# A sixth pair of up-projections with seven products, in a layer bound by TensorE

## The chip, the cores and the metric

The kernel runs on one core of one Trainium2 chip. The metric is the device time of one launch in microseconds (us), the median of several runs. TensorE (PE) does the matrix products, VectorE (DVE) and ScalarE (ACT) prepare operands and drain results, GpSimd (POOL) does some elementwise work and issues some DMAs, SyncE (SP) issues most DMAs.

## The reference, cut to what matters

One layer is computed for 512 tokens of width 1024: forgetting attention with 16 heads, a layer norm, a gated FFN with a causal convolution, a second layer norm, and a gated embedding. All of it is float32. The change sits in the FFN's first product and in what is done for it ahead of time.

```python
def conv_ffn(x, w_up, conv_w, conv_b, w_down):
    u, g = jnp.split(x @ w_up, [FFN_DIM], axis=-1)      # FFN_DIM = 2816 = 22 slices of 128
    g = causal_dwconv(g, conv_w, conv_b)                # 3 taps along the tokens
    return (jax.nn.gelu(g, approximate=False) * u) @ w_down
...
mix = fox_mixer(x, ...)                                 # q, k, v, forget gate; 16 heads
x = layer_norm(ALPHA * x + mix, ...)
x = layer_norm(ALPHA * x + conv_ffn(x, ...), ...)
x = x + sigmoid(x @ ple_w_gate + ple_b_gate) * (p @ ple_w_proj)
```

## The kernel before

**Products.** Every float32 product is made of three matmuls in a rounded format: each operand is cut into a high and a low part, and `three` (L152) adds high-high, high-low and low-high. A weight unit of up to 128x1024 is loaded into a `raw` buffer, ACT copies it to `whi` (L123), DVE subtracts to get `wlo` (L129). `W.get(i, ahead)` cuts all units up to i + ahead and starts their loads; the five `whi`/`wlo` buffers take turns.

**Stages.** V is projected in three groups of heads (`value_rows(0)` to `(2)`), with the forget gate's running sum `cr` between groups 0 and 1. Then come the loop over heads (h = 0 to 17, two steps behind the last head to drain), the output projection and the first norm. After that the 22 slices of the FFN are done as 11 pairs j = 0 to 10; slice f has a gate product g and an up product u. Between the steps of a pair PE does pieces ("chunks") of the down projection of earlier pairs, whose sums are called x, y and z, in two buffers each (x00, x01). The second norm and the embedding gate end the kernel.

**Pairs with seven products.** A plain pair (function `up`) does g and u of both slices with moving operands of 512 columns: 4 products of 8 slices of the width, 3 matmuls each, 96 in all. A pair listed in `UP_PAIRS` treats the two slices and the two halves of the width and of the tokens as a 2x2 block product and does seven half-size products instead of eight: `up_step` runs steps st = 0 to 3 for s = 0 (g) and s = 1 (u), with 256 columns, 56 x 3 = 168 matmuls. For this the weights are needed in added and subtracted form. Pairs in `KEPT` have these sums made ahead, while the heads run: `keep_load` loads the two weight blocks `ka` and `kb` and stores the sums of the previous ones to DRAM, `keep_sums` makes four subtractions on DVE (L489 to L492). `ka` has one buffer, so the next load waits for the last store; `kb` takes one of the `raw` buffers. Each pair has two sets, q = 0 and 1.

In a step, ACT and DVE move partial results from PSUM to the buffer `E` and to a corner called `side`. Step 0 of u ends with a DVE addition into `side` (L852, `side<-u,side`), without which step 1 of u cannot start, since it goes on in the same bank. After the last step `conv_product` does the convolution on ACT and DVE (L789 to L792) and the gelu and product (L797, L798). `operand_sums` (L885 to L888, four DVE additions) and `operand_parts` (L893, L894) prepare the results as operands of the down projection. For pairs in `APART`, the last two are done for the pair before, inside step 0 of this pair's u.

**Order.** From slice 2 of the FFN on, the order of DVE and ACT is the order in which the code is written; each engine works through its instructions in order. Before that a scheduler places the instructions by readiness. A numbered name is one tile: whi80 is the high part of the weight unit 80.

The lines that hold PE back are in these functions:

Of the kernel before, what the change touches and what calls it, by code (L numbers as in the profile page):

```python
# [24 lines left out]
KD = D // P  # L25
# [5 lines left out]

CHUNKS = (None, (1,) * 12, (1,) * 12, (2, 1) * 4)

UP_PAIRS = (2, 3, 4, 6, 7, 9)

KEPT = (3, 4, 6, 7)

DMA_PAIRS = (1, 2)

APART = (2, 3, 4, 7)  # L40
HALF = S // 2
ALPHA = 2.0 ** 0.25
EPS = 1e-5
# [99 lines left out]
def trunk_layer(ctx: ExitStack, tc: tile.TileContext, xT, x2d, pT, w0, wqk, wv1, wv2, bf, wo, wup, cwb,  # L143
                wdn, wpl, wg, bg, gm, bm, gf, bff, out):
    nc = tc.nc
# [21 lines left out]
    W = Weights(tc, base)  # L167
# [117 lines left out]
    u_up, u_dn = {}, [[] for _ in PAIRS]  # L285
# [87 lines left out]
    def cut_x(k, c=slice(0, S)):  # L373
        if k == 1 or c.stop == HALF:
            nc.vector.tensor_copy(xh[:, k, c], xraw[k][:, c])
        else:
            nc.scalar.activation(xh[:, k, c], xraw[k][:, c], AF.Copy)
        return nc.vector.tensor_sub(xl[:, k, c], xraw[k][:, c], xh[:, k, c].bitcast(F32)).ins
# [17 lines left out]

    proj = {}

    def value_rows(n):
        h0, nh = V_HEADS[n]  # L400
        w = VF if n == 0 else wv[n].shape[1]
        pv = [bank(f"pv{t}_{n}") for t in range(NT)]
        if n == 0:
            for s in range(2):
                proj[0, s] = bank(f"pp0_{s}")
        for k in range(KD):
            if n == 0:
                if k + 4 < KD:
                    load_x(k + 4)
                if 0 < k < KD - 1:  # L410
                    cut_x(k + 1)
                hi, lo = W.get(u_0[k + 1])
                c = slice(0, VF)
            else:
                u, c = u_v[n, k]
                hi, lo = W.get(u)
            def some(ts):
                for t in ts:
                    tk = slice(t * P, (t + 1) * P)
                    three(pv[t][:, :w], hi[:, c], lo[:, c], xh[:, k, tk], xl[:, k, tk], k == 0,  # L420
                          k == KD - 1, weights_move=True)

            def first_pair(qh, ql, c0, b):
                for s in range(2):
                    a = slice(c0 + s * P, c0 + (s + 1) * P)
                    three(proj[0, s][:, b], qh[:, a], ql[:, a], xh[:, k, b], xl[:, k, b],
                          k == 0 and b.start == 0, k in (0, KD - 1), lo_first=k > 0,
                          on=k > 0 or b.start > 0)

            if n == 0 and k == 0:  # L430
                qh, ql = W.parts[u_0[0]]
                for i in range(2):
                    first_pair(qh, ql, 0, slice(i * HALF, (i + 1) * HALF))
                    some((2 * i, 2 * i + 1))
            else:
                some((0,))
                if n == 0:
                    first_pair(hi, lo, VF, slice(0, S))
                some((1, 2, 3))
            if n == 0 and k == 0:  # L440
                with tc.issue_after(cut_first):
                    cut_x(1)
        for t in range(NT):
            if n == 0:
                logits[t] = fl_all[:, t * H:t * H + H]
                nc.scalar.activation(logits[t], pv[t][:, nh * DH:w], AF.Copy)
            v = V[:, t, h0:h0 + nh]
            p3 = pv[t][:, :nh * DH].rearrange("p (h d) -> p h d", d=DH)
            nc.scalar.activation(v[:, :, 0, :], p3, AF.Copy)
            nc.vector.tensor_sub(v[:, :, 1, :], p3, v[:, :, 0, :].bitcast(F32))  # L450
# [13 lines left out]

    to_keep, in_work, made, last_sum, last_mask = list(kept.items()), [], [], [], []

    def keep_load():

        if made:
            to, ab = made.pop()  # L470
            for n, t in enumerate(ab):
                nc.sync.dma_start(to[:, 2 * n:2 * n + 2, :], t.rearrange("p (a b) -> p a b", b=512))
        if to_keep:
            (j, q), to = to_keep.pop(0)
            ab = (ap.tile([P, UNIT], F32, name=f"ka{j}_{q}", tag="keep", bufs=1),
                  base.tile([P, UNIT], F32, name=f"kb{j}_{q}", tag="raw", bufs=RAW_BUFS))
            for n, t in enumerate(ab):
                nc.sync.dma_start(t.rearrange("p (a b) -> p a b", b=P), wup[2 * j + n, 1 - q])
            in_work.append((to, ab))
# [158 lines left out]

    stack(0)
    keep_load()  # L640
    value_rows(1)
    stack(1)
    keep_sums()
    keep_load()
    value_rows(2)
    for h in range(H + 2):
        m, s = divmod(h, 2)
        if h == 2:
            project(2, 0)
        if h < H:  # L650
            scores(h)

            if s == 0 and h != 2:
                keep_sums()
                keep_load()
        if m + 1 < KD and h != 2:
            project(m + 1, s)
        for k in OUT_FIRST.get(h, ()):
            out_first(k)
        if s == 1 and h + 1 < H:  # L660
            stack(h + 1)
        if 1 <= h < H + 1:
            turn(h - 1)
        if h >= 2:
            values(h - 2)
        if s == 1 and h + 1 < H:
            stack(h + 2)
        if h == H:
            y = base.tile([P, NT, D], F32, tag="xh", name="y")
            for t in range(NT):  # L670
                nc.sync.dma_start(y[:, t, :], x2d[t * P:(t + 1) * P, :])
# [150 lines left out]
    def up_step(j, st, s, E, amid=None):  # L822
# [4 lines left out]
            ups[j, s] = bank(f"{'gu'[s]}{2 * j}", "two" if j > 2 else None)  # L827
        ps = ups[j, s]
        z, x = ps[:, :HALF], ps[:, HALF:]
        hi, lo = W.get(u_up[j, st, s], 4)  # L830
        first, second = slice(0, HALF), slice(HALF, S)

        def go(to, col, on, a=None, sn=None, last=4):
            for k in range(4):
# [4 lines left out]
                    mh, ml = [v[:, a[0] + k, a[1]] for v in (x1h, x1l)]  # L839
                three(to, hi[:, w], lo[:, w], mh, ml, k == 0 and not on, k == 3, on=on)  # L840

        e = E[:, (1 - s) * 2 * S:(2 - s) * 2 * S]
        c1 = side(7)[:, s * HALF:(s + 1) * HALF]
        if st == 0:
            go(z, 1, False, a=(4, first))
            go(x, 0, True, a=(0, first))
            nc.scalar.activation(c1, z, AF.Copy)
            nc.scalar.activation(z.rearrange("p (a b) -> p a b", b=P),
                                 zeros.unsqueeze(1).to_broadcast([P, 2, P]), AF.Copy)
            if amid is not None:  # L850
                amid()
            nc.vector.tensor_add(c1 if j in APART else e[:, :HALF], x, c1)  # L852
        elif st == 1:
            go(z, 0, True, sn=0)
            go(x, 1, True, sn=1)
            nc.scalar.activation(e[:, S:S + HALF], x, AF.Copy)
            nc.scalar.activation(e[:, S + HALF:], z, AF.Copy)
            if j in APART:
                nc.scalar.activation(e[:, :HALF], c1, AF.Copy)
        elif st == 2:  # L860
            go(z, 1, True, sn=3)
            go(x, 0, True, sn=2)
            nc.vector.tensor_add(e[:, S:], ps, e[:, S:])
        else:
            go(x, 0, True, a=(4, second))
            del ups[j, s]
            nc.scalar.activation(e[:, HALF:S], x, AF.Copy)

    def conv_product(fs, E):

# [370 lines left out]
```

## Time and profile before

| | |
|---|---|
| runs | 645.18, 645.60, 645.79 us; median 645.6 us |
| the profiled execution | 645.37 us; its span in the trace 643.5 us |
| PE busy | 638.3 us of the span, 3635 matmuls, granted clock 1.00 |
| DVE busy | 532.4 us, 863 instructions |
| ACT busy | 383.4 us, 682 instructions |
| POOL busy | 127.6 us |
| DMA | 121.08 MB, mean 188 GB/s |

Times below are in us from the start of the span. A row of the timeline gives start, duration, engine, line, operation and the tiles written and read; "x2" means two instructions drawn as one row. In brackets stands the idle time of the engine before it and what ended it. Durations of successive instructions on one engine overlap in the trace, so the work of a chain is the distance between starts. Busy time in a window says how much an engine did there.

### The profile page before, as it was taken

The numbers are of one execution on the slowest core, as the hardware profiler recorded it, in microseconds if no ns is written. First come the engines' busy times: TensorE is split into PE (matmuls) and PEld (weight loads), VectorE is DVE, ScalarE is ACT, GpSimd is POOL, SyncE is SP. The second block draws the span as 40 slices with busy tenths as digits, with TensorE's granted clock in tenths as the row PEclk, the third lists the DMA queues.
The fourth block names the chain that finished last, engine by engine and source line by source line (L and its number), as shares of the span: only waits on it lengthen the run. The fifth ranks groups of instructions, "written<-read, shape, count | busy, mean of one in ns | idle before, by whom it ended". The sixth has DMA issues, their size and how long they took to land.

```text
span 643.5 us, 10085 instructions
## 1 busy us (share of the span) xinstructions
PE 638.3 (99%) x3635; PEld 560.6 (87%) x3635; DVE 532.4 (83%) x863; ACT 383.4 (60%) x682; POOL 127.6 (20%) x147
## 2 busy tenths in 40 slices
PE   9999999999999999999999999999999999999997
PEld 7899888888888889989999988999988998888886
DVE  6576778988888599857899987889897998699997
ACT  6274777877785326945757563647555455336872
POOL 2000554454456043110000010101011001002001
PEclk9999999999999999999999999999999999999999
DMA  8763625454588387684676838765746764782732
GB/s 314 249 226 117 209 80 185 160 189 155 177 272 321 129 256 215 135 215 156 202 221 158 227 125 250 192 205 149 238 132 202 193 217 115 164 276 61 232 109 98
DMA packets 49393, 121.08 MB, mean 188 GB/s; under 512 B 4864, under 2 KB 7936, under 8 KB 49344
## 3 DMA queue, kind: packets, MB, share of 16 engines
q1 hardware_dynamic: 44400, 107.21, 49.8%
q0 software_dynamic: 4800, 13.11, 11.0%
q8 instruction: 28, 0.46, 0.3%
q14 instruction: 21, 0.17, 0.1%
q10 hardware_dynamic: 144, 0.13, 0.1%
HBM read 107.72 MB, written 18.87 MB: 197 GB/s over the span
## 4 chain that ended last, share of the span: by engine, by line
PE 97%; DMA 1%; DVE 1%; ACT 0%; issue 0%; SPq 0%; DVEq 0%
PE g L152 18%; PE u L152 18%; PE pp L152 14%; PE x L152 8%; PE pv L152 7%; PE pl L152 7%; PE z L152 4%; PE r L152 3%; PE ap L152 3%; PE o L593 3%; PE t L580 2%; PE ao L152 2%; PE y L152 2%; PE s L543 2%; PE s L545 2%; DMA y<-x2d 1%
## 5 line engine op out<-in xcount | busy, mean ns | idle before, releaser
L123 ACT ACTIVATE whi<-raw 128x1024 fp32r<-128x1024 f32 (+4 forms) x136 | 128.1, 945 | 95.0 <-PE pv L152 17.9
L129 DVE TENSOR_TENSOR wlo<-raw,whi 128x1024 fp32r<-128x1024 f32 (+4 forms) x131 | 140.0, 1076 | 27.9 <-ACT whi L123 27.2
L567 POOL TENSOR_SCALAR pr<-pr,rl 128x128 f32<-128x128 f32 (+1 forms) x64 | 75.5, 1194 | 128.1 <-DVE rl L563 125.6
L281 POOL COPY neghalf<-neghalf 128x1 f32<-128x1 f32 x16 | 9.0, 563 | 247.1 <-ACT neghalf L280 247.1
L152 PE MATMUL g<-x1h,whi 128*128 128x256 f32 (+1 forms) x168 | 54.7, 325 | 0.0
L152 PE MATMUL g<-x1l,whi 128*128 128x256 f32 (+1 forms) x168 | 54.4, 324 | 0.0
L152 PE MATMUL g<-x1h,wlo 128*128 128x256 f32 (+1 forms) x168 | 54.3, 324 | 0.0
L152 PE MATMUL u<-x1l,whi 128*128 128x256 f32 (+1 forms) x160 | 52.9, 331 | 0.0
L152 PE MATMUL u<-x1h,wlo 128*128 128x256 f32 (+1 forms) x160 | 52.9, 331 | 0.0
L152 PE MATMUL u<-x1h,whi 128*128 128x256 f32 (+1 forms) x160 | 52.9, 331 | 0.0
L152 PE MATMUL pp<-xh,whi 128*128 128x512 f32 (+1 forms) x130 | 50.7, 390 | 0.0
L152 PE MATMUL pp<-xl,whi 128*128 128x512 f32 (+1 forms) x130 | 50.7, 390 | 0.0
L152 PE MATMUL pp<-xh,wlo 128*128 128x512 f32 (+1 forms) x130 | 50.5, 390 | 0.0
L559 ACT ACTIVATE pr<-s,nm 128x128 f32<-128x128 f32 (+1 forms) x64 | 33.5, 527 | 9.1 <-DVE nm L555 8.9
L152 PEld LDWEIGHTS g<-x1h,whi 128*128 128x128 f32 x168 | 31.9, 190 | 3.4 <-issue 0.7
L152 PEld LDWEIGHTS g<-x1l,whi 128*128 128x128 f32 x168 | 31.9, 190 | 2.7
L152 PEld LDWEIGHTS g<-x1h,wlo 128*128 128x128 f32 x168 | 31.9, 190 | 2.6
L152 PEld LDWEIGHTS u<-x1l,whi 128*128 128x128 f32 x160 | 30.4, 190 | 3.0
L152 PEld LDWEIGHTS u<-x1h,whi 128*128 128x128 f32 x160 | 30.4, 190 | 3.0
L152 PEld LDWEIGHTS u<-x1h,wlo 128*128 128x128 f32 x160 | 30.4, 190 | 2.8
L123 ACT ACTIVATE whi<-side 128x512 fp32r<-128x512 f32 (+1 forms) x33 | 25.5, 782 | 10.4 <-PE u L152 3.6
L555 DVE CUSTOM_DVE_ANT_0 s<-s,mask 128x128 f32<-128x128 f32 (+1 forms) x64 | 30.1, 510 | 1.7 <-PE s L545 1.5
(636 smaller groups left out, 1870.9 us busy)
## 6 DMA issues: line engine op xcount, KB each, us to landing
raw<-wup SPq DMA_DIRECT2D x34, 512.0 KB, 9.1
raw<-wdn SPq DMA_DIRECT2D x23, 512.0 KB, 6.7
raw<-wqk SPq DMA_DIRECT2D x14, 512.0 KB, 5.8
ka<-wup SPq DMA_DIRECT2D x8, 512.0 KB
kb<-wup SPq DMA_DIRECT2D x8, 512.0 KB, 4.3
kept<-kb SPq DMA_DIRECT2D x8, 512.0 KB, 3.2
kept<-ka SPq DMA_DIRECT2D x8, 512.0 KB
raw<-wo SPq DMA_DIRECT2D x8, 512.0 KB, 4.9
```

Of the source, the lines that this page charges most:

```text
L123: self.nc.scalar.activation(hi[:, c:e], piece, AF.Copy)
L129: self.nc.vector.tensor_sub(lo[:, c:e], piece, hi[:, c:e].bitcast(F32))
L152: nc.tensor.matmul(ps, lhsT, rhs, start=start and n == 0, stop=stop and n == 2, skip_group_check=on)
L281: with tc.issue_after(nc.gpsimd.tensor_copy(small[:, m + 32:m + 33], small[:, m:m + 1]).ins):
L543: nc.tensor.matmul(ps[:, :n], QA[:, q], KA[:, :n], start=True, stop=False)
L545: nc.tensor.matmul(ps[:, :n], qb[0:68, q], kb[0:68, :n], start=False, stop=True)
L555: last_mask[:] = [nc.vector.tensor_tensor_reduce(ps[:, :w], ps[:, :w], mask[:, S - w:], -1.0, BIG, op0=ALU.add, op1=ALU.min, accum_out=nm[ ...
L559: nc.scalar.activation(pr[:, off:off + w], ps[:, :w], AF.Exp, bias=nm[:, i:i + 1], scale=-1.0, accum_out=ls[:, i:i + 1])
L567: nc.gpsimd.tensor_scalar_mul(pr[:, off:off + w], pr[:, off:off + w], rl[:, i:i + 1])
L580: nc.tensor.transpose(ps[:, w:w + P], pr[:, o:o + P], ident)
L593: nc.tensor.matmul(ps[:, q0:], V[:, j, h], p[:, o:o + w], start=j == 0 and n == 0, stop=j == NT - 1 and n == 1)
```

## The change

Pair 5 gets seven products: it joins `UP_PAIRS` and `KEPT`, and pairs 5 and 6 join `APART`. Pair 5 then has 168 matmuls of 256 columns in place of 96 of 512; over the kernel PE has 3707 matmuls instead of 3635. Two more sets of sums have to be made and stored ahead. For them sums and loads are issued in the middle of V's second group and right behind it (the stores there go to POOL's queue instead of SP's), and again in the loop at h = 16. Further, `up_step` no longer cuts the unit four ahead at its start but three ahead; the fourth is cut by `ready()` at the step's end, behind the step's copies out of PSUM.

```diff
-UP_PAIRS = (2, 3, 4, 6, 7, 9)
-KEPT = (3, 4, 6, 7)
+UP_PAIRS = (2, 3, 4, 5, 6, 7, 9)
+KEPT = (3, 4, 5, 6, 7)
...
-APART = (2, 3, 4, 7)
+APART = (2, 3, 4, 5, 6, 7)
...
-    def value_rows(n):
+    def value_rows(n, amid=None):
...
+            if amid is not None and k == KD // 2:
+                amid()
...
-    def keep_load():
+    def keep_load(queue=nc.sync):
...
-                nc.sync.dma_start(to[:, 2 * n:2 * n + 2, :], t.rearrange("p (a b) -> p a b", b=512))
+                queue.dma_start(to[:, 2 * n:2 * n + 2, :], t.rearrange("p (a b) -> p a b", b=512))
...
-    value_rows(1)
+    def keep_amid():
+        keep_sums()
+        keep_load(nc.gpsimd)
+
+    value_rows(1, keep_amid)
     stack(1)
-    keep_sums()
-    keep_load()
+    keep_amid()
     value_rows(2)
...
             if s == 0 and h != 2:
                 keep_sums()
                 keep_load()
+        elif s == 0:
+            keep_sums()
+            keep_load()
...
-        hi, lo = W.get(u_up[j, st, s], 4)
+        hi, lo = W.get(u_up[j, st, s], 3)
...
+        def ready():
+            W.get(u_up[j, st, s], 4)
...
+            ready()        # behind the copies of each of the four steps
```

Three places show what this does to the order. Lines of the new kernel are shifted: its keep sums are L491 to L494, its V copies L452, and L864, L881, L900 to L903 are the old L852, L867, L885 to L888.

**V's second group, DVE.** ka3_1 and kb3_1 are the second set of weights of pair 3; fb, fc and cr belong to the forget gate; KA and QB are heads 0 and 1; pv0_1 is the first bank of V's second group. DVE before, from the forget gate's chain on:

```order
L629 TENSOR_TENSOR fb_407<-fb_407,fa_406 16x512
L633 SCALAR_TENSOR_TENSOR fc_421<-fb_407,fz_419 16x512
L634 CAST cr_405<-fc_421 16x512
L530 TENSOR_TENSOR KA0_428<-pp0_1_154,KA0_428 64x512
L635 TENSOR_TENSOR cr_405<-fc_421,cr_405 16x512
L636 TENSOR_SCALAR cr_405<-cr_405 16x512
L637 TENSOR_SCALAR cr_405<-cr_405 16x512
L528 SCALAR_TENSOR_TENSOR QB0_391<-pp0_0_153,QA0_427 64x512
L530 TENSOR_TENSOR KA1_568<-pp0_1_154,KA1_568 64x512
L129 TENSOR_TENSOR wlo15_747<-raw15_521,whi15_746 128x1024
L528 SCALAR_TENSOR_TENSOR QB1_392<-pp0_0_153,QA1_567 64x512
L450 TENSOR_TENSOR V_111<-pv0_1_441,V_111 128x5x64
```

In the changed kernel DVE has L491, L492 (the first two sums of this set), wlo14 and the subtraction on fb in this order, and then:

```order
L493 TENSOR_TENSOR kb3_1_526<-kb3_1_526,ka3_1_525 128x512
L635 SCALAR_TENSOR_TENSOR fc_423<-fb_409,fz_421 16x512
L532 TENSOR_TENSOR KA0_430<-pp0_1_156,KA0_430 64x512
L636 CAST cr_407<-fc_423 16x512
L494 TENSOR_TENSOR ka3_1_525<-ka3_1_525,kb3_1_526 128x512
L637 TENSOR_TENSOR cr_407<-fc_423,cr_407 16x512
L638 TENSOR_SCALAR cr_407<-cr_407 16x512
L639 TENSOR_SCALAR cr_407<-cr_407 16x512
L530 SCALAR_TENSOR_TENSOR QB0_393<-pp0_0_155,QA0_429 64x512
L532 TENSOR_TENSOR KA1_580<-pp0_1_156,KA1_580 64x512
L129 TENSOR_TENSOR wlo15_759<-raw15_533,whi15_758 128x1024
L452 TENSOR_TENSOR V_113<-pv0_1_443,V_113 128x5x64
```

Two sums now stand ahead of wlo14 and two inside the chain from fb to wlo15, and QB1 has moved behind the copies of pv0_1 to pv2_1. On PE the first matmul of pv3_2, the fourth bank of V's third group, waited for QB1 to free its bank; now it waits for the copy of pv0_1. The first matmul of pv2_2 waits for KA1 in both.

**The start of pair 5, DVE.** E4 is pair 4's result, a9 and a8 its two slices, g10 and u10 the banks of pair 5, y the running sum of the down projection. Before, pair 5 is plain, and pair 4's sums follow at once on its last product on DVE:

```order
L798 TENSOR_TENSOR E4_3880<-a8_4113,E4_3880 128x512
L885 TENSOR_TENSOR E4_3880<-E4_3880 128x256
L886 TENSOR_TENSOR E4_3880<-E4_3880 128x256
L887 TENSOR_TENSOR E4_3880<-E4_3880 128x256
L888 TENSOR_TENSOR E4_3880<-E4_3880 128x256
L894 TENSOR_TENSOR a4l_4122<-E4_3880,a4h_4121 128x512
L894 TENSOR_TENSOR b4l_4124<-E4_3880,b4h_4123 128x256
L894 TENSOR_TENSOR s4l_4126<-E4_3880,s4h_4125 128x1024
```

In the changed kernel the same last product is followed on DVE by wlo80 and the step's own addition `side<-g10`, and then:

```order
L223 TENSOR_TENSOR side_2728<-side_2728 128x512
L129 TENSOR_TENSOR wlo81_4190<-raw81_4109,whi81_4189 128x1024
L699 TENSOR_TENSOR y_2406<-y_2406,x00_3478 128x512
L699 TENSOR_TENSOR y_2406<-y_2406,x01_3479 128x512
L699 TENSOR_TENSOR y_2406<-y_2406,z00_3476 128x512
L699 TENSOR_TENSOR y_2406<-y_2406,z01_3477 128x512
L129 TENSOR_TENSOR wlo82_4239<-side_2728,whi82_4238 128x512
L900 TENSOR_TENSOR E4_3902<-E4_3902 128x256
L901 TENSOR_TENSOR E4_3902<-E4_3902 128x256
L902 TENSOR_TENSOR E4_3902<-E4_3902 128x256
L903 TENSOR_TENSOR E4_3902<-E4_3902 128x256
L864 TENSOR_TENSOR side_2728<-u10_4211,side_2728 128x256
```

Ahead of `side<-u10` there now stand three cuts of weights, the addition for g, one subtraction, four additions to y and pair 4's four sums.

**The end of pair 4, ACT.** a9 and a8 are the convolution's first tap (new L797, old L789). Before:

```order
L123 ACTIVATE whi78_4070<-raw78_3976 128x1024
L867 ACTIVATE E4_3880<-g8_3780 128x256
L123 ACTIVATE whi79_4090<-raw79_3994 128x512
L867 ACTIVATE E4_3880<-u8_3836 128x256
L789 ACTIVATE a9_4109<-E4_3880,cw_2437 128x512
L789 ACTIVATE a8_4113<-E4_3880,cw_2437 128x512
L797 ACTIVATE a9_4109<-a9_4109 128x512
```

In the changed kernel, the same place on ACT:

```order
L881 ACTIVATE E4_3902<-g8_3802 128x256
L123 ACTIVATE whi78_4105<-raw78_3998 128x1024
L881 ACTIVATE E4_3902<-u8_3858 128x256
L123 ACTIVATE whi79_4125<-raw79_4041 128x512
L797 ACTIVATE a9_4132<-E4_3902,cw_2459 128x512
L797 ACTIVATE a8_4136<-E4_3902,cw_2459 128x512
L805 ACTIVATE a9_4132<-a9_4132 128x512
```

The cut of unit 79 (512 columns here) has moved from ahead of the copy of u8 to behind it, so it stands between that copy and the convolution; the cut of unit 78 has moved behind the copy of g8.

More of the change, by code (lines that the diff above doesn't have):

```diff
@@ L859, in up_step @@
                 nc.scalar.activation(e[:, :HALF], c1, AF.Copy)
+            ready()
         elif st == 2:
@@ L863, in up_step @@
             nc.vector.tensor_add(e[:, S:], ps, e[:, S:])
+            ready()
         else:
@@ L867, in up_step @@
             nc.scalar.activation(e[:, HALF:S], x, AF.Copy)
+            ready()
     def conv_product(fs, E):
```

## The prediction

> **What bounds the kernel now.** I read the page's busy table and its chain first, then windows cut at the pairs, then the timelines of PE, DVE and ACT around the three places of the change. Busy table and chain:
>
> ```profile
> PE   638.3 (99%) x3635; PEld 560.6 (87%) x3635; DVE 532.4 (83%) x863; ACT 383.4 (60%) x682; POOL 127.6 (20%) x147
> ...
> PE 97%; DMA 1%; DVE 1%; ACT 0%; issue 0%; SPq 0%; DVEq 0%
> ```
>
> PE is busy for 99% of the span and carries 97% of the chain. Every matmul less is time saved, and every wait of PE is time lost. So the question is what PE has to do in pair 5, and whether DVE, the next busiest, still delivers in time. The windows of pairs 4, 5, 6 and 9 (window, its length; busy time and instructions of PE, PEld, DVE, ACT, POOL; clock; DMA share; GB/s):
>
> ```profile
> 342.82:373.94 31.12, 31.12 (x218) 29.16 (x217) 27.80 (x39) 19.42 (x34) 2.43 (x4) 1.00 0.74 197
> 373.94:402.79 28.85, 28.85 (x129) 23.58 (x128) 23.32 (x34) 14.18 (x22) 3.06 (x4) 1.00 0.62 180
> 402.79:433.90 31.11, 31.11 (x218) 29.14 (x216) 26.11 (x38) 17.13 (x30) 2.91 (x4) 1.00 0.67 200
> 493.84:530.39 36.55, 36.55 (x241) 33.65 (x240) 35.92 (x56) 20.23 (x34) 2.22 (x4) 1.00 0.66 192
> ```
>
> In each of them PE is full. A pair with seven products loads DVE to 84 or 89%, pair 9 to 98% without PE stopping. So on average DVE has room in pair 5; what can go wrong is a single wait, at the place where DVE's work is bunched.
>
> **The products of pair 5.** What a matmul costs is the distance of starts:
>
> ```profile
> 51.55 0.28 PE L152 MATMUL pv<-whi,xh 128*128 128x256 f32 x1
> ...
> 51.91 0.28 PE L152 MATMUL pv<-whi,xh 128*128 128x256 f32 x1
> ...
> 380.32 0.39 PE L152 MATMUL x<-whi,s2l 128*128 128x512 f32 x1
> ...
> 382.13 0.39 PE L152 MATMUL u<-x1h,whi 128*128 128x512 f32 x1
> ```
>
> Three starts of 256 columns take 0.36, so 0.120 each; the last two rows are eight starts of 512 columns apart, 1.81 or 0.2267 each. 96 x 0.2267 = 21.76 leaves and 168 x 0.120 = 20.16 comes: **-1.60**. Plain pair 5 also stops once:
>
> ```profile
> 389.61 0.39 PE L152 MATMUL x<-whi,b1h 128*128 128x512 f32 x1
> 389.97 0.47 PE L152 MATMUL g<-x1h,whi 128*128 128x512 f32 x1
> 390.27 0.40 PE L152 MATMUL g<-x1l,whi 128*128 128x512 f32 x1
> ```
>
> These starts are 0.36 and 0.30 apart instead of 0.23, where g of the second slice waits for the bank that the first slice's convolution frees; with seven products this wait is not there: **-0.2**. The price of 256 columns is more than half that of 512 (0.529), which the trace includes. The Trainium skill ("TensorE: Matmul & The Clock Gate", "Wait — 56ns, not 53.3ns?") gives the start-to-start time as columns over 2.4 GHz and some 2.5 ns, an estimate of 0.1092 for 256 columns and 0.2158 for 512; by it the products would gain 2.4. The rows have 0.120, so here the page is too good, and the sum goes by the rows.
>
> **The kept sums in V's second group.** One set costs four DVE instructions (line, engine; ns min/median/max):
>
> ```profile
> L489 DVE TENSOR_TENSOR ka<-kb,ka x8: 684/685/686, 26.6 to 193.3; 128x512 f32<-128x512 f32 x8
> ...
> L492 DVE TENSOR_TENSOR ka<-ka,kb x8: 681/682/879, 30.5 to 197.6; 128x512 f32<-128x512 f32 x8
> ```
>
> about 0.7 each. Where they now stand, DVE before did this:
>
> ```profile
> 41.41 1.22 DVE L129 TENSOR_TENSOR wlo<-raw,whi 128x1024 fp32r<-128x1024 f32 x1 [0.83 <-ACT whi L123]
> 43.88 0.68 DVE L629 TENSOR_TENSOR fb<-fb,fa 16x512 f32<-16x512 f32 x1 [1.24 <-ACT fa L628]
> ...
> 48.98 0.69 DVE L530 TENSOR_TENSOR KA<-pp,KA 64x512 fp32r<-64x512 f32 x1
> 49.70 1.23 DVE L129 TENSOR_TENSOR wlo<-raw,whi 128x1024 fp32r<-128x1024 f32 x1
> 50.96 0.69 DVE L528 SCALAR_TENSOR_TENSOR QB<-pp,QA 64x512 fp32r<-64x512 f32 x1
> 51.69 1.29 DVE L450 TENSOR_TENSOR V<-pv,V 128x320 fp32r<-128x320 f32 x3
> ```
>
> From 43.88 on DVE has no gap. PE's first matmul on pv3_2 is the 51.91 row above; it needed QB1, done at 50.96 + 0.69 = 51.65, so its slack was 0.26. In the new order the first two sums fall into the idle 0.83 and 1.24; the other two lie in the gapless chain and move wlo15 from 49.70 to 51.10. The V copy of pv0_1 follows at 52.36 and takes about 0.5 (1.29 for three, overlapped); PE goes on at some 52.9: **+0.95**. Its lower bound is 0.5, if rows of the chain overlap more than before; nothing leaves it. The first scores come about 10 us later and have slack, so nothing repeats it. KA1 moves to 51.07, still ahead of pv2_2 at 51.55.
>
> This holds if ka3_1 is there when DVE comes to it. L491 may start as late as 43.88 - 1.14 - 2 x 0.7 = 41.3 (1.14 is the distance of two cuts in a row). Its load and the store that it waits for, and landing times of the kept blocks and of all raw loads (same 512 KB):
>
> ```profile
> 31.25 0.33 SPq L472 DMA_DIRECT2D kept<-ka  x1
> ...
> 36.63 0.33 SPq L478 DMA_DIRECT2D ka<-wup  x1
> ...
> DMA to landing us min/median/max: 3.0/3.2/4.3
> ...
> DMA to landing us min/median/max: 2.9/4.8/9.1
> ```
>
> With the kb loads' row (the first, nearest: same source and queue) it lands by 39.8 to 40.9, in time; with the raw loads' median at 41.4, just late; with 9.1 at 45.7, which would cost 4.4 more. The store goes to POOL's queue now. On it the stores of `out`, half that size, land so:
>
> ```profile
> DMA to landing us min/median/max: 1.8/2.3/2.5
> ```
>
> Twice that is 4.6, less than the 5.4 between the two SP rows above, so POOL's queue is not expected to be later. I take 0.05 for this, bounds 0 and 1.0. The Trainium skill has a rule against this move ("SBUF — State Buffer", "SBUF: two separate sides"): a DMA issued by GpSimd has its descriptors written there, and certain DVE operations lock it out meanwhile. Its victims would be these stores; no row before shows a POOL store beside a full DVE, so it stands as a reason for the late-load rival below.
>
> **The start of pair 5.** PE's order there is g step 0, 12 matmuls of a chunk, u step 0, 20 of g step 1, 6 of x, 4 of g, 6 of x, then u step 1: 72 x 0.120 + 24 x 0.2267 = 14.1 after the pair's start T (373.94 before). DVE must have done `side<-u10` by then. Rows for the chain:
>
> ```profile
> 341.87 1.14 ACT L123 ACTIVATE whi<-side 128x512 fp32r<-128x512 f32 x2
> ...
> 348.80 0.36 ACT L847 ACTIVATE side<-g 128x256 f32<-128x256 f32 x1
> ...
> 349.52 1.04 ACT L123 ACTIVATE whi<-raw 128x1024 fp32r<-128x1024 f32 x1
> ...
> 378.34 0.64 ACT L797 ACTIVATE a<-a 128x512 f32<-128x512 f32 x1 [0.81 <-DVE a L792]
> ...
> 353.41 0.42 DVE L885 TENSOR_TENSOR E<-E 128x256 f32<-128x256 f32 x1
> ...
> 354.87 0.42 DVE L852 TENSOR_TENSOR side<-u,side 128x256 f32<-128x256 f32 x1
> ...
> 379.01 0.69 DVE L798 TENSOR_TENSOR E<-a,E 128x512 f32<-128x512 f32 x1 [0.16 <-ACT a L797]
> ...
> 385.91 1.27 DVE L691 TENSOR_TENSOR y<-y,x 128x512 f32<-128x512 f32 x2
> ...
> 388.30 0.74 DVE L790 SCALAR_TENSOR_TENSOR a<-g,cw,a 128x511 f32<-128x511 f32 x1
> ```
>
> Pair 4's last gelu starts at T + 4.4 and, with the cut of unit 79 now ahead of the convolution (half of 1.14), at T + 5.0. Copy, zeroing and whi80 follow on ACT: 0.57 + 0.72 + 1.0 gives T + 7.3. DVE, idle since its last product (T + 6.3), then does wlo80 (1.14, T + 8.4), the addition for g (0.34), a subtraction (0.6) and wlo81 (1.14, T + 10.5), four y additions (388.30 - 385.91 = 2.4, T + 12.9), wlo82 (0.6), four sums (354.87 - 353.41 = 1.46, T + 15.0) and L852 (0.42): T + 15.4 by these distances, some 0.2 less if the last gelu overlaps. Against 14.1 that is a stall of 1.1 to 1.3; I take **+1.1**, bounds 0.3 (ACT keeping its old pace and the idle second of DVE gone) and 1.5. In pair 4 the same wait was met by DVE at 354.87 + 0.42 = 355.3 for a start of u step 1 at 342.82 + 14.1 = 356.9, 1.6 early: there the y additions stood behind it. The four y additions and the idle time are the difference.
>
> **`ready()` in the other pairs.** It moves half a cut to a whole one (0.55 to 1.04) ahead of the convolution, so the same chain is later by as much; pair 4's slack of 1.6 covers 0.55 to 1.04. Pairs 3, 6 and 7 are alike in DVE load, pair 9 is the fullest and was already near its limit. In turn PE's copies out of PSUM come earlier by the same. I take **+0.2** for all, bounds -0.3 and +1.0.
>
> **Sums at h = 16, the loads and stores.** Four more sums of pair 7 lie in a stretch where DVE has gaps of over 2 us: 0, as long as those gaps stay. Pair 5's loads grow by 1.5 MB over 29 us, about 52 GB/s above the 180 in its window; pairs 4 and 6 ran with 197 and 200: 0, and if a cut comes late it adds to the stall at the start of the pair. Pair 5's parts, now inside pair 6's step 0, follow the pattern of pairs 3 and 4: 0.
>
> **Sum.** -1.60 - 0.2 + 0.95 + 0.05 + 1.1 + 0.2 = +0.5. On the profiled execution's 645.37 that is 645.9; this execution stands 0.23 under the median of 645.6, so the median becomes 646.1.
>
> **Rivals.**
> - *DVE keeps up, faster.* Scheduling slack that I count as lost isn't: in pair 5 the four y additions don't hold u10 up, V's stall is half, and the earlier copies out of PSUM help by the lower bound above. For it speaks pair 9, which runs DVE at 98% without stopping PE; against it that 0.26 of slack can't take two sums of 0.7. -1.8 + 0.5 - 0.3 = -1.6: 644.0. It decides in pair 5: if `side<-u10` ends by T + 14.1.
> - *The late load, slower.* ka3_1 lands after 41.3, because its store waits on POOL's queue; all of DVE's chain and V's third group stand behind L491. One us late is one us of PE: 647.1 at one, 648.1 at two. By the page's rule on descriptors this is what would happen. Against it: the first store is at about 31, well ahead of the gapless stretch.
> - *Nothing gained, nothing lost.* Pair 5's products gain 1.6 and its own stall takes just this, with V's stall hidden by later waits of PE: 645.6. PE's few waits in the trace speak against hidden slack.
>
> **Chances.** The forecast with its bounds, 0.54; DVE keeps up 0.18; late load, or the other pairs stalling as well, 0.22; nothing gained 0.06. What a measurement of this kernel can tell from no change is about 0.2%, 1.3 us. Faster by more (under 644.3): most of the second case, 0.13, and 0.04 of the first. Slower by more (over 646.9): the third case's 0.20 and 0.07 of the first. Within: 0.56. The range leaves out one in ten at either end: 644.1 to 647.6.
>
> **What would show it.** The window of V's second group: a PE gap of about 1 us at the first matmul on pv3_2, ended by a V copy. Pair 5: 168 matmuls of 256 columns and 30 of 512 (28.85 - 21.76 - 0.2 is 30 x 0.2267) make 27.0, and beside them a stall of about 1 at u step 1, ended by DVE L864. No new gap over 0.3 in pairs 3, 4, 6, 7, 9. A load of ka landing after 41.3, or gaps in several pairs, would prove it wrong upward; a pair 5 of 27 us with no gap, downward.

## The result: 7.3 us slower

The changed kernel took 652.93 us (median of four runs, 652.34 to 653.99) against 645.64 us before: ratio 1.0116, 95% interval 1.01 to 1.0132. 646.1 had been predicted, with a range up to 647.6. The page of the changed kernel, PE's busy time and its chain:

```profile
PE 639.7 (98%) x3707; PEld 564.0 (87%) x3707; DVE 541.0 (83%) x879; ACT 388.8 (60%) x700; POOL 128.5 (20%) x151
...
PE 85%; DVE 9%; ACT 2%; issue 2%; DMA 1%; DVEq 0%; ACTq 0%
```

The span grew from 643.5 to 650.8. PE had 97% of the chain and has 85% now, DVE 9%. What PE waits for, all of it (engine and line, what ended the wait, us in total, times, longest):

```profile
PE u L152 <- DVE side L864: 3.2, 5, 1.3
PE warm L334 <- DVE zeros L330: 1.1, 1, 1.1
PE g L152 <- ACT side L858: 1.1, 2, 0.6
PE g L152 <- ACT E L881: 0.7, 1, 0.7
PE pv L152 <- DVE V L452: 0.5, 1, 0.5
```

Only the `warm` wait at the start was there before. The largest entry is the addition that ends step 0, and it occurs five times, not once. The waits are rounded down here, since a waiting matmul's predecessor still counts as busy; the distance of starts shows more. Windows from the first matmul of a pair to that of the next, pair 2 before, then pairs 2, 4, 5, 6 and 7 of the changed kernel:

```profile
291.55:311.70 20.15, 20.15 (x169) 20.14 (x168) 15.33 (x22) 12.74 (x22) 0.00 (x0) 1.00 0.59 196
...
293.01:315.53 22.52, 20.61 (x169) 20.25 (x168) 14.14 (x21) 11.48 (x21) 0.00 (x0) 1.00 0.46 154
346.65:378.23 31.58, 31.38 (x218) 29.23 (x217) 27.60 (x39) 19.74 (x35) 2.46 (x4) 1.00 0.74 199
378.23:407.65 29.42, 27.78 (x201) 25.76 (x199) 23.74 (x35) 17.44 (x34) 2.43 (x4) 1.00 0.68 204
407.65:440.30 32.65, 31.65 (x216) 29.19 (x217) 30.50 (x44) 20.40 (x36) 2.46 (x4) 1.00 0.68 205
440.30:471.86 31.56, 31.37 (x218) 29.23 (x217) 27.60 (x39) 19.73 (x35) 2.43 (x4) 1.00 0.69 195
```

Pair 2, where no weight and no product was changed, takes 22.52 instead of 20.15: 2.4 of the 7.3 are lost there. Pairs 4 and 7 take 0.45 more each, pair 6 1.55 more, and pair 5, which should be 1.8 shorter, is 0.6 longer. Up to V's end 1.4 are lost (the sum of all starts that come later than 0.120 and 0.2267 and the like ask: 2.72 before, 4.13 now), but only 0.8 of it where the change is, at pv3_2 in V's third group. The other 0.65 is lost in the first 10 us, before anything that was edited runs; matmuls of 464 columns there, before and in the changed kernel:

```profile
5.38 0.38 PE L152 MATMUL pv<-whi,xh 128*128 128x464 f32 x1
5.59 0.37 PE L152 MATMUL pv<-whi,xl 128*128 128x464 f32 x1
...
5.72 0.59 PE L152 MATMUL pv<-whi,xh 128*128 128x464 f32 x1
6.11 0.59 PE L152 MATMUL pv<-whi,xl 128*128 128x464 f32 x1
```

They start 0.39 apart instead of 0.21, until 6.9. Over all kernels of this document that stretch is between 0.2 us shorter and 0.8 longer than before, with PE's order the same, so it can't be put down to the change. 2.4 + 0.9 + 1.55 + 0.6 + 0.8 + 0.65 = 6.9; the rest, some 0.4, lies behind the last matmul.

**Pair 2.** ACT and DVE at the step boundary, first before, then in the changed kernel, where PE's first stalled matmul is added:

```profile
291.52 1.06 ACT L123 ACTIVATE whi<-raw 128x1024 fp32r<-128x1024 f32 x1 [2.14 <-PE u L152]
...
293.03 1.22 DVE L129 TENSOR_TENSOR wlo<-raw,whi 128x1024 fp32r<-128x1024 f32 x1
295.46 0.42 DVE L852 TENSOR_TENSOR side<-g,side 128x256 f32<-128x256 f32 x1 [1.21 <-ACT g L848]
```

```profile
296.08 0.38 ACT L858 ACTIVATE side<-g 128x256 f32<-128x256 f32 x1 [5.24 <-PE g L152]
296.50 0.39 ACT L859 ACTIVATE g<-zeros 128x256 f32<-128x256 f32 x1
296.82 1.04 ACT L123 ACTIVATE whi<-raw 128x1024 fp32r<-128x1024 f32 x1
...
297.90 1.23 DVE L129 TENSOR_TENSOR wlo<-raw,whi 128x1024 fp32r<-128x1024 f32 x1 [3.32 <-ACT whi L123]
299.04 0.42 DVE L864 TENSOR_TENSOR side<-g,side 128x256 f32<-128x256 f32 x1
...
299.56 0.35 PE L152 MATMUL g<-xsh,whi 128*128 128x256 f32 x1 [0.64 <-ACT side L858]
```

Before, ACT cut the unit while PE was still in step 0 of g, DVE had its low part by 294.3, and the addition into `side` ran as soon as ACT had zeroed the bank. Now ACT is idle for 5.24 until PE has finished, copies, zeroes, and only then cuts; DVE stands idle for 3.32 and must make the low part before the addition, since `ready()` is written ahead of it. Relative to the pair's start (291.55 and 293.01) the addition moved from 3.9 to 6.0. PE, which needs it for g's step 1, goes on at 299.56 (the profile puts that wait down to ACT's copy, which was long done; the addition ends at 299.46). The same happens to u at 303.94.

**V's third group.** DVE and PE, after, with the load that DVE waits for:

```profile
37.69 0.33 SPq L480 DMA_DIRECT2D ka<-wup  x1
...
41.55 0.69 DVE L491 TENSOR_TENSOR ka<-kb,ka 128x512 f32<-128x512 f32 x1 [0.33 <-DMA ka<-wup]
...
44.51 0.68 DVE L631 TENSOR_TENSOR fb<-fb,fa 16x512 f32<-16x512 f32 x1 [0.41 <-ACT fa L630]
...
51.43 1.23 DVE L129 TENSOR_TENSOR wlo<-raw,whi 128x1024 fp32r<-128x1024 f32 x1
52.68 1.28 DVE L452 TENSOR_TENSOR V<-pv,V 128x320 fp32r<-128x320 f32 x3
...
53.23 0.38 PE L152 MATMUL pv<-whi,xh 128*128 128x256 f32 x1 [0.53 <-DVE V L452]
```

This is the predicted wait at the predicted place: wlo15 starts at 51.43, and pv3_2 goes on when pv0_1 is copied, 0.69 later than its distance asks (the next start adds 0.1). DVE waits 0.33 for the load, but then 0.41 for ACT ahead of `fb`: in this execution the late load costs PE nothing.

**Pair 5 and the start of pair 6.** DVE at the start of pair 5 (378.23), and ACT at its end:

```profile
386.74 0.41 DVE L864 TENSOR_TENSOR side<-g,side 128x256 f32<-128x256 f32 x1
...
388.81 1.28 DVE L699 TENSOR_TENSOR y<-y,x 128x512 f32<-128x512 f32 x2
...
393.27 0.42 DVE L864 TENSOR_TENSOR side<-u,side 128x256 f32<-128x256 f32 x1
...
406.26 1.06 ACT L123 ACTIVATE whi<-raw 128x1024 fp32r<-128x1024 f32 x1 [2.01 <-DMA raw<-wdn]
407.23 0.37 ACT L881 ACTIVATE E<-g 128x256 f32<-128x256 f32 x1
```

`side<-u` starts 15.0 after the pair's start, as worked out (15.0 and L852 on top), and PE waits. Two things were not foreseen: `side<-g` is late as well (PE loses 0.57 there), and at the end ACT waits 2.01 for a load of down weights. ACT works in order, so the copy of g10 stands behind this cut, and PE waits 0.8 for g10's bank at the start of pair 6 (this counts in pair 5's length).

### The profile page after: what moved, and what is told of

It is laid out like the page before. It is cut to its first block, busy times and chain, and to the rows that moved or that the text cites. A ratio compares the mean times of both kernels' runs of the same rounds, so it can differ in the third digit from the quotient of the medians.

```text
span 650.8 us, 10299 instructions
## 1 busy us (share of the span) xinstructions
PE 639.7 (98%) x3707; PEld 564.0 (87%) x3707; DVE 541.0 (83%) x879; ACT 388.8 (60%) x700; POOL 128.5 (20%) x151
## 4 chain that ended last, share of the span: by engine, by line
PE 85%; DVE 9%; ACT 2%; issue 2%; DMA 1%; DVEq 0%; ACTq 0%
PE u L152 15%; PE pp L152 14%; PE g L152 13%; PE pl L152 7%; PE x L152 5%; PE pv L152 5%; PE r L152 3%; PE ap L152 3%; PE ao L152 3%; DVE wlo L129 3%; PE o L595 3%; PE z L152 3%; PE t L582 3%; PE s L545 2%; PE s L547 2%
## 5 line engine op out<-in xcount | busy, mean ns | idle before, releaser
L152 PE MATMUL g<-x1h,whi 128*128 128x256 f32 (+1 forms) x164 | 51.8, 316 | 0.7 <-ACT E L881 0.7
L152 PE MATMUL g<-x1l,whi 128*128 128x256 f32 (+1 forms) x164 | 51.5, 314 | 0.0
L152 PE MATMUL g<-x1h,wlo 128*128 128x256 f32 (+1 forms) x164 | 51.5, 314 | 0.0
L152 PE MATMUL u<-x1l,whi 128*128 128x256 f32 (+1 forms) x156 | 50.1, 321 | 0.0
L152 PE MATMUL u<-x1h,wlo 128*128 128x256 f32 (+1 forms) x156 | 50.1, 321 | 0.0
L152 PE MATMUL u<-x1h,whi 128*128 128x256 f32 (+1 forms) x156 | 50.1, 321 | 0.0
L152 PE MATMUL u<-xsh,whi 128*128 128x256 f32 x112 | 32.1, 286 | 3.2 <-DVE side L864 3.2
L152 PE MATMUL g<-xsh,whi 128*128 128x256 f32 x112 | 31.9, 284 | 1.1 <-ACT side L858 1.1
L152 PE MATMUL pv<-whi,xh 128*128 128x464 f32 (+2 forms) x96 | 31.5, 328 | 0.5 <-DVE V L452 0.5
L152 PE MATMUL g<-xsh,wlo 128*128 128x256 f32 x112 | 31.8, 284 | 0.0
```

The lines of the kernel that those rows point to most:

```text
L152: nc.tensor.matmul(ps, lhsT, rhs, start=start and n == 0, stop=stop and n == 2, skip_group_check=on)
```

## The experiments

Two theories were set against each other: A, that `ready()` costs the time, by putting a cut ahead of step 0's addition; B, that pair 5's own work on DVE, ACT and the DMA queues does it. Ratios are to runs of the kernel before on the same chip, with 95% intervals. Pair lengths are distances between the first matmuls of g of successive pairs, of one profiled execution each.

| kernel | us, median | before | ratio | pair 2 | 4 | 5 | 6 | 7 |
|---|---|---|---|---|---|---|---|---|
| before | 645.64 | | | 20.15 | 31.12 | 28.84 | 31.11 | 31.12 |
| changed | 652.93 | 645.64 | 1.0116 (1.01 to 1.0132) | 22.52 | 31.58 | 29.42 | 32.66 | 31.56 |
| e1_no_ready | 648.93 | 645.81 | 1.0047 (1.0029 to 1.0065) | 20.15 | 31.12 | 27.65 | 32.05 | 31.97 |
| e2_behind_add | 650.66 | 645.81 | 1.0079 (1.0054 to 1.0104) | 21.26 | 31.40 | 28.65 | 31.21 | 31.73 |
| e3_ready_alone | 649.45 | 645.81 | 1.0057 (1.004 to 1.0074) | 22.51 | 31.57 | 28.91 | 31.11 | 31.57 |
| e4_sums_alone | 647.12 | 645.81 | 1.0022 (1.0013 to 1.0032) | 20.15 | 31.12 | 28.82 | 31.11 | 31.12 |
| e5_no_amid | 653.09 | 645.72 | 1.0111 (1.009 to 1.0132) | 20.15 | 31.12 | 27.65 | 32.33 | 32.07 |
| e6_sums_first | 651.76 | 645.72 | 1.0095 (1.007 to 1.0119) | 20.15 | 31.12 | 27.51 | 31.12 | 31.12 |
| e7_gates_later | 651.94 | 645.72 | 1.0085 (1.0061 to 1.011) | 20.15 | 31.12 | 27.79 | 31.21 | 31.18 |
| e8_pool_sums | 656.43 | 645.72 | 1.0157 (1.0136 to 1.0179) | 20.15 | 31.12 | 30.12 | 31.93 | 33.35 |
| e9_third_group | 645.06 | 645.55 | 0.9993 (0.9984 to 1.0002) | 20.15 | 31.12 | 27.69 | 31.21 | 31.12 |
| e10_head_2 | 646.21 | 645.55 | 1.0012 (1.0003 to 1.0021) | 20.15 | 31.12 | 27.50 | 31.21 | 31.12 |
| e11_both | 645.24 | 645.55 | 0.9994 (0.9985 to 1.0003) | 20.15 | 31.12 | 27.51 | 31.12 | 31.12 |
| e12_sp_stores | 646.37 | 645.64 | 1.0015 (1.0006 to 1.0023) | 20.15 | 31.12 | 28.79 | 31.11 | 31.12 |

**e1_no_ready**, the change without `ready()`:

```diff
-        hi, lo = W.get(u_up[j, st, s], 3)
+        hi, lo = W.get(u_up[j, st, s], 4)
...
-            ready()        # in all four steps
```

> The changed kernel with the cut four ahead back at the start of each step, ready() gone; pair 5 with seven products and all kept sums stay. Theory A: the cut behind the copies makes the additions `side<-g` and `side<-u` of step 0 late (2.3 us in pair 2, 0.4 in pairs 4 and 7, 1.2 in pair 6, most of pair 5's), and these stalls go; left are V's stall of 0.7 and the gain of 1.8 of pair 5, with 0 to 1 at its u step 1: 644.5 to 645.5. Rival B: pair 5's own work on DVE, ACT and the DMA queues does it, and stalls of some 4 us in pairs 5 to 8 stay: 648 to 650.

Pairs 2 and 4 are back at 20.15 and 31.12, and the kernel is 4.0 us faster than the changed one: A holds for these. But 648.93 lies outside A's numbers and inside B's. Of the 3.8 by which this profile's span is above the one before, V's third group has 1.75 (DVE waits 1.79 for the load of ka3_1), pairs 6 and 7 0.9 each, so B has a part, and pair 5 gives 1.2 back; the other 1.5 lie in the first 10 us, in the first pair of the FFN (0.43) and behind the last matmul, none of which the edit touches. The cause of pair 6's loss is in ACT, at the end of pair 5 (PE ends u10 at 404.4):

```profile
406.46 1.06 ACT L123 ACTIVATE whi<-raw 128x1024 fp32r<-128x1024 f32 x1 [2.32 <-DMA raw<-wdn]
407.42 0.37 ACT L875 ACTIVATE E<-u 128x256 f32<-128x256 f32 x1
```

The same late load again; the copy of u10 and the convolution of pair 5 stand behind it, three us after PE was done, and DVE carries the delay to pair 6's `side<-u` and on to pair 7.

At the start of pair 5 (376.75), with the four sums and the four y additions in the same place as in the changed kernel, PE no longer waits for `side<-u`. DVE's wlo80 and that addition:

```profile
382.86 1.23 DVE L129 TENSOR_TENSOR wlo<-raw,whi 128x1024 fp32r<-128x1024 f32 x1 [0.35 <-ACT whi L123]
...
390.53 0.42 DVE L860 TENSOR_TENSOR side<-u,side 128x256 f32<-128x256 f32 x1
```

**e2_behind_add**, `ready()` of step 0 behind the addition:

```diff
-            ready()
             if amid is not None:
                 amid()
             nc.vector.tensor_add(c1 if j in APART else e[:, :HALF], x, c1)
+            ready()
```

> The changed kernel with ready() of step 0 moved behind the addition into `side`; the other three steps keep it behind their copies. Theory A: the step-0 stalls go, what the last step's cut delays stays (0.8 at the start of pair 6, 0.3 in pair 8): 645 to 646. Rival B: 648 to 650. Rival C, that the cut behind the copies of steps 1 to 3 is what hurts: 650 or more.

In pair 2 more than half of the loss goes (22.52 to 21.26), and pair 6 falls to 31.21. The other steps' late cuts still cost: pair 2 keeps 1.1 (a wait for `E<-g` in step 1), pairs 4 and 7 0.3 and 0.6. So the addition is the larger part in pair 2, and C, that the cuts behind steps 1 to 3 hurt too, holds for the rest. The time, 650.66, lies in C's range; 1.3 of it are V's third group in this profile, so the pairs tell more than the time. In pair 6 one cause can be set aside: ACT's wait for the down weights at the end of pair 5 (4.54 here, 2.01 in the changed kernel) ends 1.4 us before pair 6 in both, and yet pair 6 loses 0.1 here and 1.55 there. So, as far as one profile each shows it, most of its loss in the changed kernel comes from the cut ahead of its additions.

**e3_ready_alone**, the kernel before with nothing but `ready()`:

```diff
-        hi, lo = W.get(u_up[j, st, s], 4)
+        hi, lo = W.get(u_up[j, st, s], 3)
...
+            ready()        # behind the copies of each of the four steps
```

> The kernel before with only ready(): three ahead at a step's start, the fourth behind its copies; pair 5 plain, no further sums. Theory A: pair 2 loses 2.3, pairs 4 and 7 0.4 each, pair 6 up to 1.2, pair 8 0.3: 648.7 to 650.2. Rival B: 645.6 to 646.2.

A's range, B excluded as the whole cause: 3.6 us slower with pair 5 plain. Its pairs 2, 4 and 7 are those of the changed kernel to 0.01 and lose 3.3 together; pair 6, expected to lose up to 1.2, loses nothing. These are PE's waits:

```profile
PE u L152 <- DVE side L856: 1.7, 3, 1.3
...
PE g L152 <- ACT side L850: 0.6, 1, 0.6
```

Half of the 7.3 us is thus `ready()` by itself, without any seventh product.

**e4_sums_alone**, the kernel before with the sums in and behind V's second group (the same eight sets):

```diff
+    def keep_amid():
+        keep_sums()
+        keep_load(nc.gpsimd)
+
-    value_rows(1)
+    value_rows(1, keep_amid)
     stack(1)
-    keep_sums()
-    keep_load()
+    keep_amid()
```

> The kernel before with only the kept sums and loads moved into and behind V's second group, stores there on POOL's queue; the same eight sets, pair 5 plain, no ready(). If V's stall goes through to the end: 646.3 (0.7 more). If later waits hide it: 645.6.

1.3 us slower, twice the expectation, and not hidden later. The load of ka3_1 lands later here, and DVE waits for it at the head of its chain:

```profile
42.55 0.69 DVE L491 TENSOR_TENSOR ka<-kb,ka 128x512 f32<-128x512 f32 x1 [1.37 <-DMA ka<-wup]
...
45.02 0.67 DVE L631 TENSOR_TENSOR fb<-fb,fa 16x512 f32<-16x512 f32 x1
```

One us later than in the changed kernel's profile (41.55), and PE's distance of starts at pv3_2 is 1.23 over the usual, not 0.69. So 0.54 of this us reaches PE. The rest goes into the slack that the changed kernel shows ahead of `fb` (0.41) and that is used up here.

**e5_no_amid**, e1_no_ready with V as before, the missing set made at h = 17:

```diff
-    value_rows(1, keep_amid)
+    value_rows(1)
     stack(1)
-    keep_amid()
+    keep_sums()
+    keep_load()
...
-        elif s == 0:
+        else:
             keep_sums()
             keep_load()
```

> The kernel of e1_no_ready with V's second group as it was before: sums behind stack(1) only, stores on SP; the set that is then missing is made at h = 17 instead. If V's loss comes from the sums in DVE's chain (theory A): PE's waits in V's third group go, the FFN stays as in e1_no_ready (0.6 above before in pairs 5 to 7): 646.0 to 646.6, unless the later store holds up the first norm (rival: 648 and a wait between 220 and 250).

V is as before (2.50 of extra starts against 2.72), but the rival happened: DVE meets the new sums in front of the last head's `ol`, without its load.

```profile
223.84 0.69 DVE L491 TENSOR_TENSOR ka<-kb,ka 128x512 f32<-128x512 f32 x1 [3.52 <-DMA ka<-wup]
...
PE ao L152 <- DVE ol L605: 3.0, 1, 3.0
PE nt L719 <- DVE y L711: 2.8, 2, 1.4
```

Six us between the last heads and the first norm. This is what sets the times of e5 to e8; their pairs are read from the profiles.

**e6_sums_first**, e5_no_amid with pair 4's sums ahead of pair 5's step 0:

```diff
                 if q == 0:
+                    if j == 5:
+                        operand_sums(E)
                     up_step(j, 0, 0, E)
...
-                    up_step(j, 0, 1, E, (lambda: operand_sums(E)) if j in APART else None)
+                    up_step(j, 0, 1, E, (lambda: operand_sums(E)) if j in APART and j != 5 else None)
```

> e5_no_amid with pair 4's four sums ahead of pair 5's step 0 on DVE, not inside step 0 of u. If the late `side<-u` alone costs pair 5 its gain: pair 5 shortens by 0.3 and what follows goes with it, 645.2. If DVE's whole load at the start of pair 5 counts, since it frees the buffers of the next loads: the four additions to y are later instead and pairs 5 to 7 stay within 0.3 of e5_no_amid, 646 to 646.6.

Pair 5 falls only to 27.51, but pairs 6 and 7 are back at 31.12. The cut ahead of the copy of u10, which in e5_no_amid waits 2.52 for its load of down weights, does not wait here, and the copy follows 0.8 after PE is done with u10 (407.4):

```profile
407.26 1.06 ACT L123 ACTIVATE whi<-raw 128x1024 fp32r<-128x1024 f32 x1
408.22 0.37 ACT L872 ACTIVATE E<-u 128x256 f32<-128x256 f32 x1
```

**e7_gates_later**, e5_no_amid with three DMAs of the gate moved out of pairs 5 and 6:

```diff
-            if f >= 6:
+            if f >= 6 and f not in (10, 11, 12):
                 next(beside)
+            if f in (18, 19, 20):
+                next(beside)
```

> e5_no_amid with three of the 256 KB DMAs that prepare the embedding gate, issued by POOL in pairs 5 and 6, moved to pairs 9 and 10. If the DMA engines' load makes pair 6 late (ACT waiting 2.3 us for a load of down weights at the end of pair 5): that wait shortens and pairs 6 and 7 lose 0.5 less or more, 645.5. If the loads are late because their buffers are freed late: no change against e5_no_amid.

Pairs 6 and 7 are at 31.21 and 31.18, with DVE's order as in e5, and the wait of 2.52 falls to 0.21. This speaks for too many transfers at once: the late load can be relieved from DVE's side (e6) or from the queue's (e7). The order of e6 stands in e9 to e11 too, with pairs 6 and 7 at 31.12 to 31.21; for e7 one profile alone shows it, and landing times vary, so how far it helps every time stays open.

**e8_pool_sums**, e5_no_amid with the four sums of pairs 5 to 7 on POOL:

```diff
-(lambda: operand_sums(E)) if j in APART else None
+(lambda: operand_sums(E, nc.gpsimd if j > 4 else nc.vector)) if j in APART else None
```

> e5_no_amid with the four sums inside step 0 of pairs 5, 6 and 7 on POOL instead of DVE. If DVE's load at the start of these pairs is what costs (1.5 us of DVE less in each): the waits of pairs 5 to 7 fall under 0.3 each, 644.0 to 644.6. If POOL takes over 2 us for each sum, or shares DVE's way to memory: no better than e5_no_amid, 646 or more.

The second outcome, and worse. POOL needs 1.04 to 1.59 us for a sum, against 0.42 on DVE, and a DVE subtraction that runs beside the sums takes three times its length:

```profile
387.35 1.06 POOL L890 TENSOR_TENSOR E<-E 128x256 f32<-128x256 f32 x1
...
387.17 3.72 DVE L129 TENSOR_TENSOR wlo<-raw,whi 128x1024 fp32r<-128x1024 f32 x1 [0.35 <-ACT whi L123]
390.81 0.41 DVE L857 TENSOR_TENSOR side<-g,side 128x256 f32<-128x256 f32 x1
```

3.72 instead of 1.23, so the addition for g comes late and PE with it. The Trainium skill ("SBUF — State Buffer", "SBUF: two separate sides") says that a DVE operation with two inputs in SBUF and a GpSimd operation that reads SBUF block each other for a whole instruction. The stretched row agrees in kind, though by this rule the instruction that starts first goes ahead, and here the one that starts first, by 0.18, is the one held up.

**e9_third_group**, the version with both repairs: e6_sums_first, with the second set made in V's third group behind the last V copy of the second, and no set at h = 17:

```diff
+            copied = nc.vector.tensor_sub(v[:, :, 1, :], ...).ins
+            if n == 1:
+                last_mask[:] = [copied]        # keep_sums is issued behind it
...
-    value_rows(1)
+    value_rows(1, keep_amid)
     stack(1)
-    keep_sums()
-    keep_load()
-    value_rows(2)
+    value_rows(2, keep_amid)
```

> The kernel of e6_sums_first (no ready(), pair 4's sums ahead of pair 5), without the set at h = 17: the second set is made in V's third group instead, held back behind the last V copy of the second group, stores on SP. DVE's chain from fb to QB1 is then as it was before. If V's loss came from the two sums in this chain and the late load ahead of it, V and the first norm are as before and the FFN is 1.3 faster: 644.3. If the sums only push the wait to the first heads (DVE waiting for the next load at h = 0): 645 to 646.

V and the first norm are as before, the pairs close to those of e6, and PE has one new wait of 0.2 left:

```profile
PE warm L334 <- DVE zeros L330: 1.1, 1, 1.1
PE g L152 <- DVE side L861: 0.2, 1, 0.2
```

The span is 642.5 against 643.5, the median 645.06 against 645.55; the interval of the ratio, 0.9984 to 1.0002, just includes no change. Of the 1.3 that were expected the profiles show 1.0 and the medians 0.5; the profiled execution is the fastest of its eleven, and where the others lose isn't shown. It has the lowest median found, and is 7.9 us below the changed kernel.

**e10_head_2**, as e9 with V as before and the missing set at h = 2:

```diff
-            if s == 0 and h != 2:
+            if s == 0:
```

> As e9_third_group, with V as before the change and the missing set made at h = 2, where sums were left out before. If the heads have room for 2.8 us of DVE there: 644.3. If h = 2 is short on PE and DVE is late for it: a wait of 0.5 to 3 between 70 and 90, 644.8 to 647.

The second outcome: PE waits for `PTl` at h = 2, and the gain of pair 5 is gone.

```profile
PE pp L152 <- DVE PTl L586: 0.8, 1, 0.8
```

**e11_both**, e9_third_group with the edit of e7.

> e9_third_group with three of the gate's DMAs moved from pairs 5 and 6 to pairs 9 and 10. If what is left of pair 5's wait (0.55) comes from loads that share the DMA engines: up to 0.4 faster than e9_third_group; otherwise the same.

The same as e9 within the measurement (645.24 and 645.06). Pairs 5 and 6 are at 27.51 and 31.12, but so are they in e6, which has not got this edit: with pair 4's sums first, no gain by it is shown.

**e12_sp_stores**, e4_sums_alone with `keep_load()` in place of `keep_load(nc.gpsimd)`.

> The kernel of e4_sums_alone with the stores of the kept sums in V's groups on SP's queue instead of POOL's; the scheduler then spreads the four sums of the second set a little differently over the chain (one ahead of wlo14, three inside or behind it, QB1 ahead of wlo15). If POOL's queue makes ka3_1 late: its load is issued 37.0 or before and DVE doesn't wait for it, V's third group waits 0.9 or less, 646.4 or less. If the load's landing and the sums themselves are the cause: a wait of 1 to 2 as in e4_sums_alone, 646.8 to 647.6.

The first outcome by its numbers. The load of ka3_1 is issued at 36.45, not 37.4 to 37.7, DVE waits 0.21 for it, and the extra starts up to V's end are 3.03, against 4.64 in e4_sums_alone:

```profile
40.75 0.69 DVE L491 TENSOR_TENSOR ka<-kb,ka 128x512 f32<-128x512 f32 x1 [0.21 <-DMA ka<-wup]
```

But it does not show POOL's queue as the cause. Of the 1.6 that the extra starts differ, 0.6 lies in the first 10 us. DVE's last sum before the store ends 0.64 earlier for this reason (31.18 and 31.82), and this is most of the 0.92 that the load is issued earlier; POOL issues its store 0.31 after that sum, SP 0.03. From the store's issue to the load's it is 5.24 in both. The rest of DVE's gain is the landing, 4.3 instead of 5.2 us, which no run ties to a queue. The order of the sums in the chain changed too, and the intervals of e4 and e12 overlap (1.0013 to 1.0032, 1.0006 to 1.0023), so what the queue costs stays open beyond the 0.3.

## Why the prediction was wrong, step by step

- *The products, -1.60 and -0.2.* Right: steps of 24 matmuls of 256 columns take 2.88 in every kernel, and where its waits are few, pair 5 took 27.50 to 27.69; in e6, e9 and e11 the starts that stand out add up to 0.5, 0.75 and 0.5 of this, so 27.0 is left, as forecast.
- *V, +0.95 and +0.05.* Mechanism, place and releaser right (pv3_2, ended by the copy of pv0_1): 0.8 was lost there in the changed kernel, all of it by the sums. The second term came out at nothing there, but at 0.5 in e4_sums_alone by the same count, inside its bounds of 0 and 1.0; e4 was 1.3 us slower in time. The limit of 41.3 for L491 is that of the kernel before; with all of V 0.64 later (0.59 in e4) it is 41.9, so the load was in time at 41.55 and late at 42.55. "POOL's queue is not expected to be later" was off by 0.3 at the issue. From there to the next load's issue it took 5.2 to 6.2 us on POOL (changed kernel, e1, e2, e4), 5.2 and 5.4 on SP (e12, before), not the 4.6 of the working.
- *The start of pair 5, +1.1.* Right in size, wrong in its cause: `side<-u` starts 15.0 after the pair's start, and 0.7 is lost there. The working named the four y additions and the idle time. e1_no_ready has the same additions and sums, with `side<-u` 13.8 after the start, and loses next to nothing there; so it is `ready()`, by wlo80 1.3 later, that makes it a stall. Missed was `side<-g`, 0.57, by the very chain that the working listed (wlo80 at T + 7.4, the addition behind it at T + 8.5, PE there at T + 8.5).
- *`ready()`, +0.2, bounds -0.3 and +1.0.* This is the step that failed. It was priced only where a last step's cut stands ahead of the convolution, and pair 2 was not looked at. The larger price is in step 0: the cut, its wait for ACT's zeroing included, stands ahead of the addition that PE needs next. e3_ready_alone puts it at 3.6 us by the medians. 3.3 of it are found in the pairs: 2.4 in pair 2, where DVE is only 76% busy before (15.33 of 20.15), and 0.45 each in pairs 4 and 7. Its first pair is 0.5 longer too, but so it is in e1, which has no `ready()`, and not in the changed kernel, which has it; that part isn't shown to belong here. Taken out of the changed kernel, `ready()` gives 4.0 back (e1).
- *Pair 6's parts and the DMAs, 0 and 0.* Both failed: pair 6 lost 1.55 in the changed kernel and 0.9 in e1_no_ready. In e1 it is ACT's wait of 2.3 us for a load, which ends 2 us into pair 6. In the changed kernel the wait of 2.0 ends before pair 6 and costs the 0.8 at its first matmul; of the 1.55, 1.14 is at `side<-u`, behind the late cut of `ready()` (e2: 0.1 left), and e3, without pair 5's sums and parts in pair 6, loses nothing there, so it takes both. The argument that pairs 4 and 6 run at 197 and 200 GB/s was an average over a pair; the wait came in a stretch of 10 to 15 us.
- *The rivals.* The slower one named the late load alone. It cost nothing in the changed kernel's profile and 0.5 in e4's; `ready()`, which no rival named, cost seven times that.

## What to carry to other kernels

An engine that works in order turns every instruction moved behind something into a wait for all that follows: when a step's work is put behind its copies, ask for each result that another engine needs next whether it now stands behind the moved work, and ask it in the idle stages too, where PE is not slowed by DVE's load but by a single chain. Look at every stage that runs the edited code, not only at the one that the change is about. Two profiled executions can differ by most of a us where their code is the same, here in the first 10 us: look where a difference lies before putting it down to the edit. A transfer that lands just in time by its median is a loss by its spread, above all when the instruction that needs it stands at the head of an in-order chain.

## What was not expected of the hardware

Two-input additions on POOL stretched a DVE subtraction from 1.23 to 3.72 us (e8). Loads of 512 KB of the same kind landed 3.9 us (changed kernel) and 5.2 us (e4) after their issue at the same place in the program, worked out from the issues at 37.69 and 37.37 and DVE's release. The first 10 us of PE differed by up to 1 us between kernels with the same order of matmuls there (0.22 shorter than before in e5, 0.82 longer in e7).
